# A hybrid recurrent and attention layer on one core: four gate units ahead of the seven-product pairs, another order of their sums, and more low parts made by DMA

## The chip, the core and the metric

The kernel runs on one core of a Trainium2 chip. The core has five engines with their own instruction streams: TensorE (PE, matmuls; PEld is its weight load), VectorE (DVE), ScalarE (ACT), GpSimd (POOL) and SyncE (SP), which here issues most DMAs. Each runs its instructions in the order in which they were written, and waits for others by semaphores. The metric is the device time of one execution in microseconds.

## The reference

One layer for 512 tokens of width 1024, all in float32:

```python
h = rmsnorm(x, norm_w)
proj = einsum('bsd,de->bse', h, w_in) + b_in      # 11272 columns
(mq, mk, mv, mi, mf, mo, mz, sq, sk, sv, sz, gates) = split(proj)
qk = silu(causal_conv4(concat([mq, mk])))          # mLSTM branch, 4 heads of 256
hm = rmsnorm(mlstm_chunkwise(q, k, v, log_i, log_f))
y_m = hm * sigmoid(mo) * silu(mz)
qs, ks = rmsnorm(sq), rmsnorm(sk)                  # stick-breaking attention, 8 heads of 128
y_s = stick_breaking_attention(qs, ks, sv) * silu(sz)
g_m, g_s = split(sigmoid(gates))
merged = g_m * (y_m @ w_proj_m) + g_s * (y_s @ w_proj_s)
out = x + merged @ w_out
```

Nearly all the work is the product of h with w_in, and the three products behind it.

## The kernel before, in words

**Float32 products.** Each operand is split into a high part, rounded to the format that TensorE takes (float32r), and a low part, the rest. A product is three matmuls, high by high, high by low and low by high (`mm3`, lines 93 to 96, and L963 in the pairs). Splitting a weight tile (`split`, L98) costs one ACT copy for `wh` (L99) and one DVE subtraction for `wl` (L100). Units marked `by_dma` make the low part otherwise: ACT writes `wh` (L126) and the negated weight into `wl` (L127), and POOL issues a DMA that adds the weight to it (L128). The buffer of the weight, `stg`, is then free only when that DMA has landed.

**Units.** The work of TensorE is a list of units that run one after the other. A full unit is 128 columns of a weight matrix by all tokens, or 256 rows by 512 columns, 24 matmuls of 512 columns. SP loads the weight of a unit four units ahead into one of three `stg` buffers; it is split two units ahead into one of three `wh` and of three `wl`. When a unit's products are done, the next iteration of the loop evacuates them from PSUM. Iteration c of the loop emits, in this order: the evacuation of unit c − 1; all that stands in the table `later` for c; the load of unit c + 4 and the split of unit c + 2; the first half of unit c's matmuls; steps of the attention and mLSTM heads that are under way, matmuls among them; the second half. This order is the program order on every engine, and nothing reorders it.

**The pairs.** v of both branches and k of set 0 come from two *pairs*. A pair computes two groups of 512 columns by the 2 × 2 block scheme that needs seven block products in place of eight (`Pair`, `Half`). Its blocks are X, Y, Z and V (each in two halves g); each product p has two half-units of 12 matmuls, which are split two half-units ahead as any unit is. The operands are sums of the blocks. Before, the sums are Y + V (`t3`, by DMA, L1010), X + Y (`t2`, L1014), Z + X (`t4`, L1018) and X − V (`t1`, L1022), the last three on DVE, and the products run in the order 1, 2, 6, 5, 7, 3, 4. Product 1 multiplies X, 2 Z, 6 X after X + Y, 5 X after X − V, 7 Y after Y + V, 3 V, 4 Z after Z + X. The same sums of h are the tiles `form`, made by DVE and ACT while x is normalised and in the first iterations (L905, L913, L914). Products 1, 6, 7 and 4 accumulate in bank a, 2 in c, 5 and 3 in b; ACT copies a bank into `u`, DVE adds a bank to the bias row into `dst` (L1043), and POOL adds `u` to it by DMA (L1046).

**The order of the groups before** (E = 32 is the first unit behind the pairs):

| units | what |
|---|---|
| 0 to 3 | q of attention set 0 |
| 4 to 17, 18 to 31 | pair 1 (v of set 1 and v of the mLSTM pair 1), pair 2 (v and k of set 0); half-units |
| 32 to 47 | z of set 0, q, k and z of set 1, four units each |
| 48 to 51 | first half of the merge gate g_m (GM), sigmoid on ACT, stored in DRAM (`gm_park`) |
| 52 to 67 | o, z, q, k of mLSTM pair 0 |
| 68 to 87 | o, z, v, q, k of mLSTM pair 1 |
| 88 to 99 | all eight units of the gate g_s (GS) and the second half of GM, kept in tiles |
| 100 to 115 | projections w_proj_s and w_proj_m, their 16 outputs times the gates |
| 116 to 129 | the output product, again by seven products |

Evacuations of q and k of a set are additions of the bias row on DVE (L387: `qraw`, `kraw`). k of mLSTM units and q units have a causal convolution on DVE (L729, L731, L737, L746) and two ACT steps; o and z units have one or two DVE instructions. The attention heads run beside units from E + 1 on: ACT exponentials (L504), POOL selects (L506), DVE scans (L512, L513) and transposes through DRAM.

`by_dma` are units 36 to 43 (q and k of set 1) and the last eight of w_proj_m, and the two half-units of product 1 in the first pair (L946 to 948).

Of the kernel before, what the change touches and what calls it, by code (L numbers as in the profile page):

```python
# [37 lines left out]
def tile_hybrid_layer(  # L38
# [931 lines left out]
    class Pair:  # L970

        def __init__(self, c1, c2, got1, got2):
# [36 lines left out]
        def t3(self, g):  # L1009
            nc.gpsimd.dma_start(out=self.raw["Y", g], in_=self.raw["V", g], accum_op=OP.add)  # L1010

        def t2(self, g):
            x, y = self.raw["X", g], self.raw["Y", g]
            nc.vector.tensor_tensor(x, x, y, op=OP.add)  # L1014

# [565 lines left out]
```

## Time and profile before

| | before |
|---|---|
| time, median of 3 runs | 699.28 us (699.22 to 702.11) |
| the profiled execution | 699.28 us, span 697.5 us |
| granted TensorE clock, mean | 0.995 |
| busy: PE, DVE, ACT, POOL | 677.6, 489.6, 374.9, 133.0 us |
| HBM read, written | 79.85, 15.79 MB |

A timeline row has its start in us, its duration in us, the engine, the line of the program, the instruction, its output and inputs, the shape and in brackets the idle time of the engine in front of it and what ended it. A window row has, behind its length, busy time and instructions of PE, PEld, DVE, ACT and POOL, the granted clock, the mean share of the DMA engines and GB/s. A group's row ends with its busy time and the mean duration in ns. Matmuls are pipelined, so each lasts longer than the step to the next.

### The profile page before, as it was taken

The page shows a single profiled execution, that of the slowest core. Times are in us where ns is not written, and L with a number is a line of the kernel's source. Part 1 is how long each engine was busy: PE and PEld are TensorE (multiplying, and loading weights), DVE is VectorE, ACT ScalarE, POOL GpSimd, SP SyncE. Part 2 cuts the span into 40 slices and gives each one's busy share as a digit, 9 for nine tenths or more (in the row PEclk, how much of TensorE's full clock was granted, in tenths as well). Part 3 has the DMA queues.
Part 4 walks back from the last instruction along what each step waited for, and adds up shares of the span by engine and source line. Part 5 has one row for each costly group of instructions (what it writes and reads, how often), then busy time and mean ns, then how long its engine had stood idle before and what let it go on. Part 6 is the DMA issues. An engine that isn't in the chain of part 4 may idle for free.

```text
span 697.5 us, 9279 instructions
## 1 busy us (share of the span) xinstructions
PE 677.6 (97%) x3114; PEld 560.4 (80%) x3114; DVE 489.6 (70%) x849; ACT 374.9 (54%) x705; POOL 133.0 (19%) x268
## 2 busy tenths in 40 slices
PE   8998999999979999999999999999999999999997
PEld 5876868788758888888887888888888888888876
DVE  6797596765496985698987545699643375445996
ACT  7567444666845645564355564444647453344451
POOL 4157203134621221210001031100002100111020
PEclk9999999999989999999999999999999999999999
DMA  7947948579788559475355424353523349679333
GB/s 247 309 100 223 267 113 204 161 162 253 196 209 254 147 175 249 127 187 98 86 117 144 113 76 135 107 150 91 134 78 90 91 145 298 190 169 220 125 81 101
DMA packets 131503, 111.97 MB, mean 161 GB/s; under 512 B 17098, under 2 KB 105572, under 8 KB 131456
## 3 DMA queue, kind: packets, MB, share of 16 engines
q1 hardware_dynamic: 125840, 95.53, 47.6%
q0 software_dynamic: 5472, 15.73, 12.0%
q8 instruction: 24, 0.39, 0.2%
q14 instruction: 23, 0.19, 0.1%
q10 hardware_dynamic: 144, 0.13, 0.1%
HBM read 79.85 MB, written 15.79 MB: 137 GB/s over the span
## 4 chain that ended last, share of the span: by engine, by line
PE 67%; DMA 7%; DVE 6%; issue 4%; ACT 3%; SPq 2%; POOL 0%; DVEq 0%; ACTq 0%; POOLq 0%
PE dps L94 19%; PE dps L95 19%; PE dps L96 19%; PE aps L95 3%; PE aps L96 3%; PE aps L94 3%; DMA stg<-in_w_in_dram 2%; DVE acc L731 2%; DMA Y<-V 2%; DMA t_d<-ty 1%; ACT sqj L404 1%; DMA wl<-stg 1%; DVE wl L100 1%; PE aps L840 1%; PE aps L842 1%
## 5 line engine op out<-in xcount | busy, mean ns | idle before, releaser
L94 PE MATMUL dps<-hh,wh 128*128 128x512 f32 x448 | 176.6, 394 | 4.2 <-DVE kraw L387 4.1
L96 PE MATMUL dps<-hh,wl 128*128 128x512 f32 x448 | 175.5, 392 | 0.5 <-DVE wl L100 0.5
L95 PE MATMUL dps<-hl,wh 128*128 128x512 f32 x448 | 175.4, 392 | 0.0
L100 DVE TENSOR_TENSOR wl<-stg,wh 128x1024 fp32r<-128x1024 f32 x68 | 83.2, 1223 | 59.9 <-ACT wh L99 59.7
L94 PEld LDWEIGHTS dps<-hh,wh 128*128 128x128 f32 x448 | 84.8, 189 | 21.7 <-issue 4.5
L96 PEld LDWEIGHTS dps<-hh,wl 128*128 128x128 f32 x448 | 84.7, 189 | 18.9 <-DVE wl L100 1.0
L95 PEld LDWEIGHTS dps<-hl,wh 128*128 128x128 f32 x448 | 84.8, 189 | 16.7
L99 ACT ACTIVATE wh<-stg 128x1024 fp32r<-128x1024 f32 x68 | 71.6, 1052 | 28.4 <-PE dps L95 20.6
L512 DVE TENSOR_TENSOR_SCAN om<-om 128x512 f32<-128x512 f32 (+3 forms) x32 | 27.0, 845 | 19.6 <-POOL om L506 19.6
L94 PE MATMUL dps<-wh,hh 128*128 128x512 f32 x96 | 37.6, 392 | 1.3 <-DVE qraw L387 1.3
L734 ACT ACTIVATE tmp<-acc 128x512 f32<-128x512 f32 x16 | 10.1, 633 | 52.3 <-DVE acc L731 52.3
L95 PE MATMUL dps<-wl,hh 128*128 128x512 f32 x96 | 37.5, 391 | 0.3 <-DMA wl<-stg 0.3
L96 PE MATMUL dps<-wh,hl 128*128 128x512 f32 x96 | 37.4, 390 | 0.0
L731 DVE SCALAR_TENSOR_TENSOR acc<-tmp,vec,acc 128x511 f32<-128x511 f32 (+2 forms) x48 | 36.0, 750 | 1.7
L126 ACT ACTIVATE wh<-stg 128x1024 fp32r<-128x1024 f32 x16 | 16.9, 1058 | 30.5 <-PE dps L95 15.5
L128 POOL DMA_DIRECT2D wl<-stg x16 | 14.1, 881 | 99.8 <-ACT wl L127 44.7
L506 POOL TENSOR_SCALAR_AFFINE_SELECT om<-om 128x128 f32<-128x128 f32 x32 | 16.4, 517 | 66.3 <-ACT om L504 49.2
L793 POOL TENSOR_SCALAR_AFFINE_SELECT w_all<-om 128x128 f32<-128x128 f32 x16 | 7.3, 491 | 108.3 <-DMA om<-rb_d 108.3
L94 PE MATMUL dps<-yh,wh 128*128 128x512 f32 x64 | 24.9, 389 | 0.0
L95 PE MATMUL dps<-yl,wh 128*128 128x512 f32 x64 | 24.9, 389 | 0.0
L96 PE MATMUL dps<-yh,wl 128*128 128x512 f32 x64 | 24.9, 389 | 0.0
L504 ACT ACTIVATE om<-aps,rq 128x512 f32<-128x512 f32 (+3 forms) x32 | 16.9, 528 | 12.7 <-PE aps L96 11.7
(302 smaller groups left out, 1555.2 us busy)
## 6 DMA issues: line engine op xcount, KB each, us to landing
stg<-in_w_in_dram SPq DMA_DIRECT2D x71, 512.0 KB
wl<-stg POOLq DMA_DIRECT2D x16, 512.0 KB, 5.9
a_d<-ay SPq DMA_DIRECT2D x8, 640.0 KB
az<-a_d SPq DMA_DIRECT2D x32, 160.0 KB
stg<-in_w_proj_s_dram SPq DMA_DIRECT2D x8, 512.0 KB
B<-in_w_out_dram SPq DMA_DIRECT2D x8, 512.0 KB
stg<-in_w_proj_m_dram SPq DMA_DIRECT2D x8, 512.0 KB
dst<-u POOLq DMA_DIRECT2D x12, 256.0 KB, 5.6
```

What stands on the lines that cost most here:

```text
L94: nc.tensor.matmul(ps, ah, bh, start=first, stop=False)
L95: nc.tensor.matmul(ps, ah, bl, start=False, stop=False)
L96: nc.tensor.matmul(ps, al, bh, start=False, stop=last)
L99: nc.scalar.activation(hi, src, AF.Copy)
L100: nc.vector.tensor_tensor(lo, src, hi.bitcast(F32), op=OP.subtract)
L126: nc.scalar.activation(self.wh, self.st, AF.Copy)
L128: nc.gpsimd.dma_start(out=self.wl, in_=self.st, accum_op=OP.add)
L504: nc.scalar.activation(om[:, 0:n], zp, AF.Sigmoid, scale=rn[:, h:h + 1])
L506: nc.gpsimd.affine_select(out=om[:, ts], in_=om[:, ts], compare_op=OP.is_gt, fill=1.0, base=0, channel_multiplier=1, pattern=[[-1, 128]])
L512: nc.vector.tensor_tensor_scan(back, back, back, 1.0, op0=OP.mult, op1=OP.bypass)
L731: nc.vector.scalar_tensor_tensor(acc[:, j:], t[:, 0:T - j], cw(3 - j, ch), acc[:, j:], op0=OP.mult, op1=OP.add)
L734: nc.scalar.activation(t, acc, AF.Sigmoid)
```

## The change

1. Four units (`FILL`), the first half of GS, stand between q of set 0 and the first pair. So the pairs are units 8 to 21 and 22 to 35, and E is 36. With them both pairs are loaded by a plan of due units, and the `form` sums and splits are made over iterations 2 to 7.
2. The pairs' products run in the order 1, 2, 5, 6, 7, 3, 4. The sums are X + Y (DVE, one iteration ahead of the pair), Y + V (DMA, one behind its start), X + V (DVE, three behind), Z + X (DVE, four behind). Product 5 takes X after the first sum, 6 after X + V. Products 6 and 7 now follow each other on bank a.
3. Product 1 of the first pair is split as all others.
4. The `by_dma` units are E + 4 to E + 19: z of set 1 and the first half of GM too. The low part of v of mLSTM pair 0, which returns from DRAM, is made in the same way.
5. z of mLSTM pair 0 alternates with q of that pair (`weave`): o, q, z, q, z, q, z, q, z, k.
6. All sixteen gate tiles are stored in DRAM behind their sigmoid (`park`) and come back at four places between the last gate unit and the eighth unit behind (`gate_back`). Buffers of that stretch change: the early splits of y_s go into `qk` tiles, two splits of y_m move to later units, and the loads and sums of the output product's weights move by one to four units.
7. The turn of q of set 0 goes from E − 9 to E − 6, the gates' scan from E + 24 to E + 26.

```diff
-E = 4 + 14 * PAIRS
+FILL = 4
+E = 4 + FILL + 14 * PAIRS
...
-GATES_PREP, GATES_START, GATES_SCAN = E - 3, E - 1, E + 24
+GATES_PREP, GATES_START, GATES_SCAN = E - 3, E - 1, E + 26
...
-            later.setdefault(E - 9, []).append(fn) if name == "q" else defer(2, fn)
+            later.setdefault(E - 6, []).append(fn) if name == "q" else defer(2, fn)
...
+            if not self.p:
+                nc.scalar.activation(vl, t, AF.Copy, scale=-1.0)
+                nc.gpsimd.dma_start(out=vl.rearrange("p h e -> p (h e)"), in_=t.rearrange("p h e -> p (h e)"), accum_op=OP.add)
+                return lambda: None
...
-            if self.pair.base == 4 and self.p == 1:
-                nc.scalar.activation(self.wh, x, AF.Copy)
-                nc.scalar.activation(self.wl, x, AF.Copy, scale=-1.0)
-                nc.gpsimd.dma_start(out=self.wl, in_=x, accum_op=OP.add)
-            else:
-                split(x, self.wh, self.wl)
+            split(x, self.wh, self.wl)
...
-            for p in (1, 2, 6, 5, 7, 3, 4):
+            for p in (1, 2, 5, 6, 7, 3, 4):
...
+                if first:
+                    plan = {"X": b - 6 + g, "Z": b - 3 + 3 * g, "V": b - 3 + g, "Y": b - 4 + g}
+                else:
+                    plan = {"X": b - 6 + g, "Z": b - 7 + 5 * g, "V": b - 3 + g, "Y": b - 6 + g}
...
-                self.at(b + g - 2, self.t3, g)
-                self.at(b + 1 + g, self.t2, g)
-                self.at(b + 3 + g, self.t4, g)
-                self.at(b + 4 + g, self.t1, g)
+                for n, (z, y, dma) in enumerate((("X", "Y", False), ("Y", "V", True),
+                                                   ("X", "V", False), ("Z", "X", False))):
+                    self.at(b + (-1, 1, 3, 4)[n] + g, self.sum, z, y, g, dma)
...
+    def park(dst, o, n=0):
+        def evac(ct, ps):
+            ct += n
+            t = blk("tmp", name="gpark")
+            nc.scalar.activation(t, ps, AF.Sigmoid, bias=bias(o + ct))
+            nc.sync.dma_start(dst[128 * ct:128 * ct + 128, :], t)
+        return evac
+
+    gs_park, gm_park = [dp.tile([D, T], F32, name=n) for n in ("gs_park", "gm_park")]
+    chan_group(w_in, C_GS, 512, h_mov, park(gs_park, 48))
...
+    weave(16, 0, 1, 2, 3, 8, 4, 9, 5, 10, 6, 11, 7, 12, 13, 14, 15)
...
-    gate_group(C_GS, 48, D, gs_tile)
-    gate_group(C_GM + 512, 44, 512, gm_late)
+    chan_group(w_in, C_GS + 512, 512, h_mov, park(gs_park, 48, 4))
+    chan_group(w_in, C_GM + 512, 512, h_mov, park(gm_park, 40, 4))
...
-    for un in units[n_proj - 8:] + units[E + 4:E + 12]:
+    for un in units[n_proj - 8:] + units[E + 4:E + 20]:
         un.by_dma = True
...
-    at_unit(n_gates + 3, gm_back)
+    at_unit(n_gates - 1, gate_back, gs_park, gs_t, 0, ("brow", "om", "om", "acc"))
+    for n in (0, 2):
+        at_unit(n_gates + 2, gate_back, gs_park, gs_t, 4 + n)
+        at_unit(n_gates + 4, gate_back, gm_park, gm_t, n)
+        at_unit(n_gates + 8, gate_back, gm_park, gm_t, 4 + n)
```

Three places of DVE's program are shown. Line numbers of the changed kernel differ: its split is L101, its sums are L1011.

The start of the first pair, before: `form` are the sums of h, `Z`, `X` the blocks, `dst` the first output.

```order
L100 TENSOR_TENSOR wl<-Z,wh 128x1024
L1014 TENSOR_TENSOR X<-X,Y 128x1024
L914 SCALAR_TENSOR_TENSOR form<-h_368,form 128x512
L914 SCALAR_TENSOR_TENSOR form<-h_349,form 128x512
L100 TENSOR_TENSOR wl<-Z,wh 128x1024
L1014 TENSOR_TENSOR X<-X,Y 128x1024
L914 SCALAR_TENSOR_TENSOR form<-h_352,form 128x512
L100 TENSOR_TENSOR wl<-X,wh 128x1024
L1018 TENSOR_TENSOR Z<-Z,X 128x1024
L100 TENSOR_TENSOR wl<-X,wh 128x1024
L1043 TENSOR_TENSOR dst<-prow,aps 128x512 x2
```

The same place now:

```order
L101 TENSOR_TENSOR wl<-X,wh 128x1024
L1011 TENSOR_TENSOR X<-X,Y 128x1024
L919 SCALAR_TENSOR_TENSOR form<-h_283,form 128x512
L919 SCALAR_TENSOR_TENSOR form<-h_286,form 128x512
L101 TENSOR_TENSOR wl<-X,wh 128x1024
L1011 TENSOR_TENSOR X<-X,Y 128x1024
L101 TENSOR_TENSOR wl<-Z,wh 128x1024 x2
L101 TENSOR_TENSOR wl<-X,wh 128x1024
L1011 TENSOR_TENSOR X<-X,V 128x1024
L101 TENSOR_TENSOR wl<-X,wh 128x1024
L1032 TENSOR_TENSOR dst<-prow,aps 128x512 x2
L1011 TENSOR_TENSOR Z<-Z,X 128x1024
```

X + Y stands ahead of both low parts of product 2's Z, and X + V behind the first low part of product 5's X.

The evacuation of k of set 1 (`kraw`), before: the rows above it are the last of head 1 (scans `om`, transposes `ay`) and two low parts of z units.

```order
L431 STREAM_TRANSPOSE ty<-qraw 128x8x32 x4
L100 TENSOR_TENSOR wl<-stg,wh 128x1024
L100 TENSOR_TENSOR atl<-az,ath 128x512
L100 TENSOR_TENSOR atl<-az,ath 128x384
L530 STREAM_TRANSPOSE ay<-a_all 128x4x32 x10
L512 SCALAR_TENSOR_TENSOR om<-om 128x256
L513 TENSOR_TENSOR a_all<-a_all,om 128x256
L512 SCALAR_TENSOR_TENSOR om<-om 128x384
L513 TENSOR_TENSOR a_all<-a_all,om 128x384
L100 TENSOR_TENSOR wl<-stg,wh 128x1024
L387 TENSOR_TENSOR kraw<-dps,brow 128x512 x4
```

The same place now:

```order
L432 STREAM_TRANSPOSE ty<-qraw 128x8x32 x4
L101 TENSOR_TENSOR atl<-az,ath 128x512
L101 TENSOR_TENSOR atl<-az,ath 128x384
L531 STREAM_TRANSPOSE ay<-a_all 128x4x32 x10
L513 SCALAR_TENSOR_TENSOR om<-om 128x256
L514 TENSOR_TENSOR a_all<-a_all,om 128x256
L513 SCALAR_TENSOR_TENSOR om<-om 128x384
L514 TENSOR_TENSOR a_all<-a_all,om 128x384
L388 TENSOR_TENSOR kraw<-dps,brow 128x512 x4
```

Both subtractions are gone from DVE; nothing else moved there.

Units of q of mLSTM pair 0 on DVE, before one after the other (`acc` and `tmp` are the convolution, `ys` a head's output):

```order
L100 TENSOR_TENSOR wl<-stg,wh 128x1024
L729 TENSOR_SCALAR acc<-tmp,vec 128x512
L731 SCALAR_TENSOR_TENSOR acc<-tmp,vec,acc 128x511
L731 SCALAR_TENSOR_TENSOR acc<-tmp,vec,acc 128x510
L731 SCALAR_TENSOR_TENSOR acc<-tmp,vec,acc 128x509
L746 TENSOR_TENSOR mqt<-tmp,mqt 128x512
L100 TENSOR_TENSOR atl<-az,ath 128x384
L737 SCALAR_TENSOR_TENSOR tmp<-acc,tmp 128x512
L100 TENSOR_TENSOR wl<-stg,wh 128x1024
```

Now with a z unit's two instructions (L718, L719) between:

```order
L730 TENSOR_SCALAR acc<-tmp,vec 128x512
L732 SCALAR_TENSOR_TENSOR acc<-tmp,vec,acc 128x511
L732 SCALAR_TENSOR_TENSOR acc<-tmp,vec,acc 128x510
L732 SCALAR_TENSOR_TENSOR acc<-tmp,vec,acc 128x509
L747 TENSOR_TENSOR mqt<-tmp,mqt 128x512
L101 TENSOR_TENSOR atl<-az,ath 128x512
L101 TENSOR_TENSOR atl<-az,ath 128x384
L718 SCALAR_TENSOR_TENSOR tmp<-dps,bvec,tmp 128x512
L719 SCALAR_TENSOR_TENSOR ym<-tmp,vec,ym 128x512
L101 TENSOR_TENSOR wl<-stg,wh 128x1024
```

Between two convolutions now stand a z unit's evacuation and its low part.

More of the change, by code (lines that the diff above doesn't have):

```diff
@@ L1007, in load, with sum @@
             nc.sync.dma_start(t, w_in[r:r + 256, c:c + 512].rearrange("(k p) c -> p k c", p=128))
[L1009 to L1014, printed above, removed]
-        def t4(self, g):
-            z, x = self.raw["Z", g], self.raw["X", g]
-            nc.vector.tensor_tensor(z, z, x, op=OP.add)
-        def t1(self, g):
-            x, v = self.raw["X", g], self.raw["V", g]
-            nc.vector.tensor_tensor(x, x, v, op=OP.subtract)
+        def sum(self, z, y, g, dma):
+            z, y = self.raw[z, g], self.raw[y, g]
+            if dma:
+                nc.gpsimd.dma_start(out=z, in_=y, accum_op=OP.add)
+            else:
+                nc.vector.tensor_tensor(z, z, y, op=OP.add)
         def rows(self):
@@ L1075, in at_unit @@
         later.setdefault(c, []).append(lambda: fn(*a))
-    at_unit(1, units[4].split)
-    for f in (5, 7, 6):
-        for i in range(2):
-            at_unit(2, form_sum, f, i)
-    for f, c in ((6, (3, 4)), (5, (4, 5)), (7, (5, 6)), (3, (9, 10))):
+    for n, c in enumerate((2, 2, 2, 2, 3, 3)):
+        at_unit(c, form_sum, (5, 7, 6)[n // 2], n % 2)
+    for f, c in ((5, (4, 4)), (6, (5, 5)), (7, (6, 6)), (3, (7, 7))):
         for i in range(2):
@@ L1094, in tile_hybrid_layer, with weave @@
     sets[1].z_group()
-    gm_park = dp.tile([512, T], F32, name="gm_park")
-    def gm_early(ct, ps):
-        t = blk("tmp", name="gmp")
-        nc.scalar.activation(t, ps, AF.Sigmoid, bias=bias(40 + ct))
-        nc.sync.dma_start(gm_park[128 * ct:128 * ct + 128, :], t)
-    chan_group(w_in, C_GM, 512, h_mov, gm_early)
+    chan_group(w_in, C_GM, 512, h_mov, park(gm_park, 40))
+    def weave(n, *order):
+        b = len(units) - n
+        units[b:] = [units[b + i] for i in order]
     pairs[0].o_group()
@@ L1111, in tile_hybrid_layer, with gate_back @@
     pairs[1].qk_group("k", C_MK, 8)
-    gs_t, gm_t = [], [None] * 8
-    def gs_tile(ct):
-        if ct < 4:
-            tag = ("brow", "om", "om", "acc")[ct]
-            gs_t.append(blk(tag, shape=(516 if tag == "om" else 512,), name="gs")[:, 0:512])
-        elif ct % 2 == 0:
-            gs_t.extend(two("qk", name="gs"))
-        return gs_t[ct]
-    def gm_back():
-        for n in range(2):
-            t = blk("qk", F32, (2, 512), name="gm")
-            nc.sync.dma_start(t, gm_park[256 * n:256 * n + 256, :].rearrange("(i p) t -> p i t", p=128))
-            for i in range(2):
-                gm_t[2 * n + i] = t[:, i, :]
-    def gm_late(ct):
-        if ct % 2 == 0:
-            gm_t[4 + ct:6 + ct] = two("qk", name="gm")
-        return gm_t[4 + ct]
-    def gate_group(c0, o, n, tile_of):
-        def evac(ct, ps):
-            nc.scalar.activation(tile_of(ct), ps, AF.Sigmoid, bias=bias(o + ct))
-        chan_group(w_in, c0, n, h_mov, evac)
-    gate_group(C_GS, 48, D, gs_tile)
-    gate_group(C_GM + 512, 44, 512, gm_late)
+    gs_t, gm_t = [None] * 8, [None] * 8
+    def gate_back(src, dst, n, tags=None):
+        if tags:
+            for i, tag in enumerate(tags):
+                dst[n + i] = blk(tag, shape=(516 if tag == "om" else 512,), name="gback")[:, 0:512]
+                nc.sync.dma_start(dst[n + i], src[128 * (n + i):128 * (n + i) + 128, :])
+        else:
+            t = blk("qk", F32, (2, 512), name="gback")
+            nc.sync.dma_start(t, src[128 * n:128 * n + 256, :].rearrange("(i p) t -> p i t", p=128))
+            for i in range(2):
+                dst[n + i] = t[:, i, :]
+    chan_group(w_in, C_GS + 512, 512, h_mov, park(gs_park, 48, 4))
+    chan_group(w_in, C_GM + 512, 512, h_mov, park(gm_park, 40, 4))
     n_gates = len(units)
@@ L1486, in tile_hybrid_layer @@
     for k in range(8):
-        later.setdefault(n_gates + 3 + k // 2, []).append(
+        later.setdefault(n_gates + (3 + k // 2 if k < 6 else 8), []).append(
             y_late(y_m, ymp, k, k) if k < 5 else y_own(k))
@@ L1534, in tile_hybrid_layer @@
             x_turn(2)
-            units[5].split()
         for g in list(act):
```

34 lines of the change are left out of this document (14 added, 20 removed).

## The prediction

> **What bounds the kernel now.** I read the page's busy shares and its chain of waits first.
>
> ```profile
> PE 677.6 (97%) x3114; PEld 560.4 (80%) x3114; DVE 489.6 (70%) x849; ACT 374.9 (54%) x705; POOL 133.0 (19%) x268
> PE 67%; DMA 7%; DVE 6%; issue 4%; ACT 3%; SPq 2%; POOL 0%; DVEq 0%; ACTq 0%; POOLq 0%
> ```
>
> TensorE is busy for 97% of the span, and the change leaves it the same products. So only the time in which it waits can be won. The timeline of PE gives every such wait behind the start-up (in brackets: the idle time and what ended it); the first and third row stand before and behind one of them, and the row at 263.92, which waits for nothing, is used further on.
>
> ```profile
> 43.08 0.39 PE L963 MATMUL aps<-wh,hh 128*128 128x512 f32 x1
> 43.90 0.50 PE L963 MATMUL aps<-wl,hh 128*128 128x512 f32 x1 [0.44 <-DVE wl L100]
> 44.24 0.40 PE L963 MATMUL aps<-wh,hl 128*128 128x512 f32 x1
> ...
> 52.53 0.50 PE L963 MATMUL aps<-wh,form 128*128 128x512 f32 x1 [0.24 <-ACT wh L99]
> 54.85 0.50 PE L963 MATMUL aps<-wl,form 128*128 128x512 f32 x1 [1.82 <-DVE wl L100]
> 58.40 0.50 PE L963 MATMUL aps<-wl,form 128*128 128x512 f32 x1 [0.53 <-DVE wl L100]
> 62.43 0.50 PE L963 MATMUL dps<-wl,form 128*128 128x512 f32 x1 [0.76 <-DVE wl L100]
> 95.83 0.50 PE L963 MATMUL aps<-wh,form 128*128 128x512 f32 x1 [0.26 <-ACT wh L99]
> 97.09 0.50 PE L963 MATMUL aps<-wl,form 128*128 128x512 f32 x1 [0.76 <-DVE wl L100]
> 100.67 0.50 PE L963 MATMUL aps<-wl,form 128*128 128x512 f32 x1 [0.56 <-DVE wl L100]
> 132.42 0.33 PE L481 MATMUL aps<-ident,dst 128*128 128x128 f32 x1 [0.80 <-DVE dst L419]
> 133.20 0.55 PE L481 MATMUL aps<-ident,dst 128*128 128x128 f32 x3 [0.46 <-DVE dst L419]
> 176.18 0.50 PE L94 MATMUL dps<-wh,hh 128*128 128x512 f32 x1 [1.30 <-DVE qraw L387]
> 195.81 0.50 PE L95 MATMUL dps<-wl,hh 128*128 128x512 f32 x1 [0.27 <-DMA wl<-stg]
> 205.40 0.77 PE L94 MATMUL dps<-hh,wh 128*128 128x512 f32 x1 [4.09 <-DVE kraw L387]
> 263.92 0.39 PE L94 MATMUL dps<-hh,wh 128*128 128x512 f32 x1
> 380.80 0.50 PE L96 MATMUL dps<-hh,wl 128*128 128x512 f32 x1 [0.52 <-DVE wl L100]
> ```
>
> A wait costs more than its idle time. Matmuls follow each other by some 0.23 us (44.24 − 43.90 is 0.34); around the wait of 0.44 us two steps take 44.24 − 43.08 = 1.16 in place of 0.46, so 0.70 are lost: the idle time and 0.26 more. The long wait at 205.40 costs clock too, which the view by short windows shows (PEclk is the column behind the engines).
>
> ```profile
> 203.00:204.00 1.00, 0.00 (x0) 0.00 (x0) 1.00 (x2) 0.00 (x0) 0.00 (x0) 0.83 1.07 313
> ...
> 210.00:211.00 1.00, 1.00 (x5) 0.82 (x4) 0.85 (x1) 0.00 (x0) 0.02 (x1) 0.76 1.14 342
> ```
>
> All rows between them have 0.50. A mean of 0.83 is half speed from 203.66 on, and 0.76 ends it at 210.48. The idle time began at 205.40 − 4.09 = 201.31, so the clock fell 2.35 us into it. From 205.40 to 210.48 half speed cost 5.08 / 2 = 2.5 us. With 0.26 for each wait, the losses are: first pair 3.79 + 5 × 0.26 = 5.1; second pair 1.58 + 0.78 = 2.4; at head 0, 1.26 + 0.52 = 1.8; before k of set 1, 1.56; the DMA's, 0.53; at 205.40, 4.09 + 0.26 + 2.5 = 6.85; at 380.80, 0.78. Together 19.0 us. The profiled execution took 699.28 us, which is the median of the runs itself, so the sum is made against 699.28 and its least possible end is 680.3.
>
> **The pairs.** Two rows of the chain say what the pairs and head 0 wait for besides DVE, two windows and two groups what DVE and PE have to do there.
>
> ```profile
> 75.58 11.96 DMA Y<-V
> 114.72 9.38 DMA stg<-in_w_in_dram
> ```
>
> ```profile
> 40.00:60.00 20.00, 16.98 (x71) 12.56 (x70) 18.45 (x21) 12.22 (x36) 16.34 (x7) 1.00 0.32 95
> 580.00:600.00 20.00, 20.00 (x90) 16.56 (x89) 12.60 (x16) 7.26 (x11) 0.00 (x0) 1.00 0.87 275
> ```
>
> ```profile
> L1043 DVE TENSOR_TENSOR dst<-prow,aps 128x512 f32<-128x512 f32 x8 | 5.1, 684 | 0.0
> L1022 DVE TENSOR_TENSOR X<-X,V 128x1024 f32<-128x1024 f32 x4 | 4.9, 1225 | 0.0
> ```
>
> Before, Y + V (the DMA of 11.96 us) stands ahead of X + Y, on which products 6, 5 and 4 depend, and DVE is busy 18.45 of 20 us around 50. After, X + Y needs loads alone, and Y + V goes out in the second half-unit of the pair and is read by the ninth. 90 matmuls in 20 us are 0.222 each, so a half-unit of 12 is 2.67 us; its split runs two half-units ahead, which leaves five of them, 13.4 us, for a transfer of 11.96. The fullest half-unit for DVE is now the fifth: two adds into dst, two sums and one subtraction, 2 × 0.68 + 3 × 1.22 = 5.0 us at most, against the two half-units (5.33 us) by which splits run ahead. So DVE just keeps up if it enters it without a lag. In the first pair four squares of a q norm stand ahead of ACT's copy there, and DVE has done two subtractions more than before, since the first pair's low parts are no longer made by DMA. I take 1.0 us of stalls for the first pair (bounds: 0, and the 5.1 of before with those two subtractions, 7.5) and 0.3 for the second (0 to 2.4). **Gain: 4.1 + 2.1.**
>
> The four gate units ahead of the pairs are the same TensorE work at another place: 24 matmuls of a unit and one subtraction of 1.2 us each, on a DVE that a full unit (5.3 us) leaves idle most of the time; their sigmoids (one ACT instruction for each) go into the two tmp buffers and from there to DRAM by SP. At head 0 the load of 9.38 us came late behind the second pair's loads, and the k norm's scale behind it on ACT, in order. The pair's loads now stand at other units and less together; I take 0.3 of the 1.8 as left (0 to 1.8). **Gain: 1.5.**
>
> **Sixteen low parts by DMA.** Before k of set 1 is evacuated, DVE works without a gap from 189 us; four rows of it:
>
> ```profile
> 196.52 1.19 DVE L100 TENSOR_TENSOR wl<-stg,wh 128x1024 fp32r<-128x1024 f32 x1
> 197.63 1.15 DVE L100 TENSOR_TENSOR atl<-az,ath 128x512 fp32r<-128x512 f32 x2
> ...
> 203.44 1.22 DVE L100 TENSOR_TENSOR wl<-stg,wh 128x1024 fp32r<-128x1024 f32 x1
> 204.57 1.88 DVE L387 TENSOR_TENSOR kraw<-dps,brow 128x512 f32<-128x512 f32 x3
> ```
>
> The two subtractions are low parts of the first two z units behind it, and both leave DVE. They take 1.11 and 1.13 us of its time (197.63 − 196.52 and 204.57 − 203.44), so kraw starts at 202.33 and PE idles 4.09 − 2.24 = 1.85 us. That ends 0.50 us ahead of the point at which the clock fell, and the wait of 1.82 us at 54.85 stands in a window with the clock at 1.00. What is left is 1.85 + 0.26 = 2.1 us. **Gain: 4.7.** The wait at 176.18 has nothing moved ahead of it and stays.
>
> [...]
>
> The price is on ACT and POOL: the second copy, and the issue of the transfer.
>
> ```profile
> L127 ACT ACTIVATE wl<-stg 128x1024 fp32r<-128x1024 f32 x16 | 16.7, 1044 | 0.0
> L128 POOL DMA_DIRECT2D wl<-stg x16: 850/864/947, 139.9 to 641.0; - x16
> DMA to landing us min/median/max: 4.5/6.1/8.5
> ```
>
> The four low parts of pair 0's v go the same way, two of the pairs' no longer do, so POOL issues ten more transfers. One low part takes 2 × 1.04 + 0.86 + 6.1 = 9.0 us from its split, at most 2.9 + 8.5 = 11.4. The eight new units ran from 205.40 to 263.92 (the row of that time is the first matmul behind them), without the 2.5 us of lost clock 7.0 each, so two of them are 14.0 us of lead. The transfers hide, by 2.6 us even with the longest of these rows. The buffer stg comes free only on landing, and three of them serve all: load, copies, issue and landing have three units, 21.0 us, against 9.38 + 2.1 + 0.9 + 8.5 = 20.9. I take the one late wait of before (0.53) and 0.8 for the new ones (bounds: 0 and the rival C below). **Loss: 0.8.**
>
> **z woven with q.** In the second half of the program DVE lags behind four convolutions in a row, and one wait (0.78) comes of it. Placing a z unit, which gives DVE two instructions beside its low part where a q unit gives five, between q units takes that lag out in steps; I take half, with 0 and 0.78 as ends. **Gain: 0.4.**
>
> **Gates parked in DRAM.** Sixteen tiles of 256 KB cross to DRAM and back in place of four: 3 MB more stored, over the whole program, and 3 MB more loaded, within nine units behind the last gate unit, where the projections' weights are loaded too.
>
> ```profile
> 20.00:40.00 20.00, 20.00 (x94) 16.39 (x93) 16.02 (x37) 13.13 (x30) 3.66 (x4) 1.00 1.06 305
> 600.00:620.00 20.00, 20.00 (x90) 16.58 (x89) 6.25 (x9) 8.55 (x9) 3.37 (x4) 1.00 0.75 184
> 620.00:640.00 20.00, 20.00 (x90) 16.57 (x89) 12.32 (x20) 8.84 (x11) 2.73 (x4) 1.00 0.91 197
> ```
>
> At 305 GB/s, the fullest window, 3.15 MB take 10.3 us of all DMA engines. The windows from 580 to 640 have shares of 0.87, 0.75 and 0.91, so 0.47 × 20 = 9.4 us are free there. The loads of the last weights start one to four units later and make room, so that it need cost nothing; if none of the free time can be used it costs 10.3. I take what is over, 0.9. **Loss: 0.9.**
>
> **The sum:** 4.1 + 2.1 + 1.5 + 4.7 + 0.4 − 0.8 − 0.9 = 11.1, and 699.28 − 11.1 = **688.2 us**.
>
> **The rivals.** *A: the clock still falls.* ACT makes each z unit's second copy (1.04 us) in the same stretch, in order, ahead of the exponentials that DVE's scans wait for. If that delays kraw by over 0.50 us, PE idles past 2.35 us and half speed follows, 2.5 us, with up to 1.0 us of wait: 688.2 + 3.5 = 691.7. For it: the margin of 0.50 is small beside the 2.24 on which it rests. Against it: at 189 to 204 DVE ran without a pause, so it was DVE's own work that was late.
>
> *B: the pairs' stalls only move.* The sums are as many as before, DVE has two subtractions more in the first pair, and products 6 and 7 now share a bank back to back, with a copy by ACT between them that PE must wait for. If 6.2 of the pairs' gain is gone, 688.2 + 6.2 = 694.4. For it: 18.45 of 20 us busy in the first pair. Against it: the chain went through Y + V, and the change takes it off the way to products 5 and 6.
>
> *C, on the other side: the three stg buffers become the bound in the eight new units.* With a landing as the pairs' (11.96 us) in place of 8.5, the round of load, copies, issue and landing is 9.38 + 3.0 + 11.96 = 24.3 us for three units of 21.0: 1.1 us lost a unit, 8.8 in all, 697.0. It decides from a round of 26.5 us on, 2.2 us above these longest rows: there (26.5 − 21.0) / 3 × 8 = 14.7 us go and the result passes 702.8; with 27.5 us 17.3 are lost and it is **705.5**. For it: SP waits for the buffer in order, so loads of other tiles (the transposes' round through DRAM, the parked v) come later as well, and gate stores are added to its queue. Against it: eight units in a row already work so before the change, with one wait of 0.27.
>
> [...]
>
> **How the numbers follow.** About 0.5%, 3.5 us, is what a measurement of this kernel can tell from no change: faster is below 695.8, slower above 702.8. The forecast has 0.47 (its own range 684 to 692, by the pairs' and the buffers' bounds), A 0.14, B 0.19, C 0.14 (half of it above 702.8), and 0.06 lie with the crowded end of the program, up to 688.2 + 9.4 = 697.6. Faster: 0.47 + 0.14, 0.14 of B (the rest where losses at the buffers join it) and 0.04 of the last: 0.79. Slower: half of C and a little of B: 0.08. Same: 0.13. The range goes from 681, all but nothing of the 19.0 left, to 699.
>
> **What would show it.** X + Y of each pair ending while its product 1 runs; Y<-V landing without anyone waiting; no idle over 1 us within the pairs. DVE going from its transposes to kraw without a low part between, PE idle there near 1.85, the granted clock 1.00 in that window. 24 issues of wl<-stg by POOL in place of 16, and landings under 9 us. No new idle time in the last 130 us. The forecast is wrong if PE waits for "DMA wl<-stg" in the GM units, if the clock shows 0.50 near k, or if waits for DVE's low parts sum to more than 3 us in the pairs.

## The result and the profile after

The changed kernel takes 694.93 us (median of 20 runs, 692.87 to 700.82) against 699.29 us (20 runs) of the kernel before: a ratio of 0.9941, with a 95% interval of 0.9927 to 0.9955. It is 4.4 us faster; 11.1 were forecast, and 694.93 lies within the range of 681 to 699 but at less than half of the gain. The profiled execution took 695.85 us, 3.4 less than that of before.

The timeline of PE of the changed kernel has these waits behind the start-up; it answers the list in the prediction (L101 is now the split, L388 the evacuation of `kraw`, L482 the first matmul of head 0).

```profile
68.72 0.50 PE L963 MATMUL aps<-wl,form 128*128 128x512 f32 x1 [0.50 <-DVE wl L101]
75.72 0.50 PE L963 MATMUL dps<-wl,form 128*128 128x512 f32 x1 [1.25 <-DVE wl L101]
149.88 0.33 PE L482 MATMUL aps<-ident,dst 128*128 128x128 f32 x1 [2.47 <-DVE dst L420]
150.66 0.55 PE L482 MATMUL aps<-ident,dst 128*128 128x128 f32 x3 [0.46 <-DVE dst L420]
193.66 0.50 PE L95 MATMUL dps<-wh,hh 128*128 128x512 f32 x1 [1.30 <-DVE qraw L388]
213.29 0.50 PE L96 MATMUL dps<-wl,hh 128*128 128x512 f32 x1 [0.28 <-DMA wl<-stg]
220.41 0.47 PE L95 MATMUL dps<-hh,wh 128*128 128x512 f32 x1 [1.61 <-DVE kraw L388]
233.47 0.50 PE L97 MATMUL dps<-hh,wl 128*128 128x512 f32 x1 [0.19 <-DMA wl<-stg]
259.78 0.50 PE L96 MATMUL aps<-ktt,qtt 128*128 128x512 f32 x1 [0.52 <-DVE ktt L101]
301.21 0.50 PE L96 MATMUL aps<-ktt,qtt 128*128 128x512 f32 x1 [1.92 <-DVE ktt L101]
607.70 0.50 PE L97 MATMUL dps<-yh,wl 128*128 128x512 f32 x1 [0.25 <-DMA wl<-stg]
```

The second pair has no wait left, the first one 1.75 us; `kraw` waits 1.61 in place of 4.09. But head 0 waits longer than before (2.47 and 0.46 in place of 0.80 and 0.46), and two waits are new, both in front of the attention heads' first product (`ktt`, at 259.78 and 301.21). With 0.26 us for each wait, as in the prediction, against its losses of before:

| place | before | after | forecast for after |
|---|---|---|---|
| pairs | 7.5 | 2.3 | 1.3 |
| head 0 | 1.8 | 3.5 | 0.3 |
| before k of set 1 (`qraw`) | 1.6 | 1.6 | 1.6 |
| low parts by DMA near 213 and 233 | 0.5 | 1.0 | 1.3 |
| `kraw` with its clock | 6.85 | 1.9 | 2.1 |
| `ktt` with its clock | 0 | 4.7 | 0 |
| behind the convolutions | 0.8 | 0 | 0.4 |
| the end | 0 | 0.5 | 0.9 |
| sum | 19.0 | 15.5 | 7.9 |

The sums fall by 3.5 us, the profiled executions by 3.4. The clock part of `ktt` is from the view by windows of the changed kernel:

```profile
302.00:303.00 1.00, 1.00 (x8) 0.89 (x7) 1.00 (x2) 0.00 (x0) 0.00 (x0) 0.80 0.00 0
...
306.00:307.00 1.00, 1.00 (x5) 0.83 (x5) 0.00 (x0) 0.00 (x0) 0.00 (x0) 0.99 0.01 3
```

Half speed lasts from 302.60 (a mean of 0.80) to 306.02 (0.99), 3.42 us, and costs half of that, 1.7. Two misses make up the difference: 3.2 us at head 0 and 4.7 at `ktt`.

**Head 0.** The chain of waits of the changed kernel ahead of 149.88:

```profile
132.16 8.16 DMA stg<-in_w_in_dram
140.40 1.07 ACT wh L100
142.36 4.18 DMA stg<-in_w_in_dram
146.65 1.07 ACT wh L100
149.74 0.88 DVE dst L420 x4
```

Two weight loads came late, one after the other, ACT waited for each in order, and the scale of k's norm (`dst`) on DVE came behind. The timeline of SP says why:

```profile
128.07 0.60 SPq L120 DMA_DIRECT2D stg<-in_w_in_dram  x1
128.72 3.34 SPq L440 DMA_DIRECT2D t_d<-ty  x4
132.16 0.57 SPq L120 DMA_DIRECT2D stg<-in_w_in_dram  x1
139.01 3.31 SPq L445 DMA_DIRECT2D tz<-t_d  x4
142.36 0.58 SPq L120 DMA_DIRECT2D stg<-in_w_in_dram  x1
```

L440 and L445 are the turn of q of set 0, which the change moves from E − 9 to E − 6: four stores to DRAM and four loads back, which wait until the stores have landed. From 132.7 to 139.0 SP issued nothing: it stood in front of the four loads of L445, and the weight load behind them was issued at 142.36.

**`ktt`.** Ahead of 301.21 the chain is made of the same kind of piece:

```profile
240.07 11.08 DMA stg<-in_w_in_dram
260.64 8.30 DMA stg<-in_w_in_dram
273.81 5.99 DMA vback<-v_park
294.02 1.04 ACT wh L100
```

and the view of waits of the changed kernel names what ACT waited for before its copies of weights (total in us, times, longest), over the whole program:

```profile
ACT wh L100 <- DMA stg<-in_w_in_dram: 12.8, 5, 4.2
ACT wh L127 <- DMA stg<-in_w_in_dram: 4.7, 3, 2.4
```

Between 230 and 303 us it is 6.4 us in two waits of the first kind and all of the second.

So my theory after the result was: SP's order at head 0; and at `ktt` the sixteen low parts by DMA, which hold the three `stg` buffers until they land, so that loads of later units start late, ACT waits for them in order, and the heads' steps behind ACT come late on DVE. The rivals: full DMA engines in both places, or the gate stores and the returning v in SP's queue.

### The profile page after: what moved, and what is told of

Read it like the earlier page. It is cut to its first block, busy times and chain, and to the rows that moved or that the text cites. A ratio compares the mean times of both kernels' runs of the same rounds, so it can differ in the third digit from the quotient of the medians.

```text
span 693.7 us, 9384 instructions
## 1 busy us (share of the span) xinstructions
PE 676.1 (97%) x3114; PEld 559.9 (81%) x3114; DVE 480.6 (69%) x839; ACT 383.5 (55%) x715; POOL 130.0 (19%) x278
## 4 chain that ended last, share of the span: by engine, by line
PE 66%; DMA 13%; DVE 6%; issue 6%; ACT 5%; POOL 2%; SPq 2%; ACTq 0%; DVEq 0%; POOLq 0%
PE dps L97 16%; PE dps L95 16%; PE dps L96 16%; DMA stg<-in_w_in_dram 5%; PE dps L963 4%; DMA wl<-stg 3%; DMA vback<-v_park 2%; PE aps L963 2%; PE aps L96 2%; PE aps L97 2%; DMA stg<-in_w_proj_m_dram 2%; PE aps L95 2%; ACT sqj L405 1%; DVE wl L101 1%; PE dps L1438 1%
## 5 line engine op out<-in xcount | busy, mean ns | idle before, releaser
L101 DVE TENSOR_TENSOR wl<-stg,wh 128x1024 fp32r<-128x1024 f32 x60 | 73.4, 1224 | 55.9 <-ACT wh L100 55.8
L129 POOL DMA_DIRECT2D wl<-stg x24 | 21.1, 879 | 103.1 <-ACT wl L128 72.7
L128 ACT ACTIVATE wl<-stg 128x1024 fp32r<-128x1024 f32 x24 | 25.1, 1047 | 0.0
L101 DVE TENSOR_TENSOR atl<-az,ath 128x384 fp32r<-128x384 f32 (+1 forms) x24 | 13.9, 607 | 15.1 <-ACT ath L100 8.7
```

Of the source, the lines that this page charges most:

```text
L101: nc.vector.tensor_tensor(lo, src, hi.bitcast(F32), op=OP.subtract)
L128: nc.scalar.activation(self.wl, self.st, AF.Copy, scale=-1.0)
L129: nc.gpsimd.dma_start(out=self.wl, in_=self.st, accum_op=OP.add)
```

## The experiments

All times are medians, of four runs for most kernels, with the ratio to runs of the kernel before on the same chip. The intervals of two of these kernels that lie within some 2 us of each other mostly overlap; there the waits in the profiles carry the reading, and not the difference of the medians.

### 1. The turn of q back at E − 9

```diff
-            later.setdefault(E - 6, []).append(fn) if name == "q" else defer(2, fn)
+            later.setdefault(E - 9, []).append(fn) if name == "q" else defer(2, fn)
```

> The changed kernel with one edit undone: the turn of q of set 0 goes back from E - 6 to E - 9. Theory (SP's queue): the turn's sixteen small DMAs, eight of which wait for the others to land, stand in SP's queue ahead of the weight loads of the units behind the pairs, ACT waits for those loads in order, and the scale of k's norm is late behind it. Then the wait of PE for 'DVE dst' at head 0 (2.47 + 0.46 us of idle time in the changed kernel's profile) falls to that of the kernel before (0.80 + 0.46) or below, and the time falls by 1.7 to 3.4 us against the changed kernel's 694.9, to 691.5 to 693.2. Rival (the pair's loads or the DMA engines' load make those loads late, wherever the turn stands): the wait stays at 2.5 or more, the time at 694.9.

690.90 us, ratio 0.9872 (0.9854 to 0.989): 4.0 less than the changed kernel. No wait at head 0 is left, of 2.93. That is the theory, and more than it promised: the two waits for `ktt` are still there, but of other lengths and without the clock's fall, which had cost 1.7 us.

```profile
217.29 0.47 PE L95 MATMUL dps<-hh,wh 128*128 128x512 f32 x1 [1.86 <-DVE kraw L388]
257.35 0.50 PE L96 MATMUL aps<-ktt,qtt 128*128 128x512 f32 x1 [1.70 <-DVE ktt L101]
297.68 0.50 PE L96 MATMUL aps<-ktt,qtt 128*128 128x512 f32 x1 [0.83 <-DVE ktt L101]
```

### 2. Ten units' low parts by DMA in place of sixteen

```diff
-    for un in units[n_proj - 8:] + units[E + 4:E + 20]:
+    for un in units[n_proj - 8:] + units[E + 4:E + 14]:
```

> The changed kernel with low parts by DMA for E + 4 to E + 13 only, ten units in place of sixteen: the first two z units keep it, the other two and the four gate units get DVE's subtraction back. Theory (stg): the low-part DMAs hold the three stg buffers until they land and fill the DMA engines, so the later loads start late, ACT waits for them in order, and the heads' rows come late on DVE. Then the waits at 233, 260 and 301 us (0.19, 0.52 and 1.92 us idle, with half clock behind the last) go, kraw stays at some 1.6 us, and the time falls by 4 to 5 us to 690 to 691. Rival (the parked v's return and the gate stores in SP's queue make the wait at 301 us): that wait stays at about 1.9 us, and the time at 694 to 695.

692.73 us, ratio 0.9904 (0.987 to 0.9937), with a profiled execution of 690.65. The waits for `ktt` are gone, though the returning v and the gate stores still stand in SP's queue, so that rival falls as a cause by itself; `kraw` waits for 1.71 us. The median fell by 2.2 us, less than expected; the profiled execution fell by 5.2 against that of the changed kernel (695.85) although half speed struck at head 0, which is still late here:

```profile
149.20 0.48 PE L482 MATMUL aps<-ident,dst 128*128 128x128 f32 x1 [2.17 <-DVE dst L420]
```

### 3. Both edits

> Both edits together: the turn of q at E - 9 and ten units' low parts by DMA. If both causes are as said and do not touch each other, the gains add up to 6 to 8 us: 687 to 689, about the forecast of 688.2, with waits of PE behind the start-up of 7 us or less. If they share one cause (full DMA engines), the two together gain no more than the better of them, 690 to 691.

688.42 us, ratio 0.9836 (0.9814 to 0.9858): 6.5 less than the changed kernel, about the sum of the first two (4.0 and 2.2), and at the forecast of 688.2. The two causes are separate. Its waits behind the start-up:

```profile
68.50 0.50 PE L963 MATMUL aps<-wl,form 128*128 128x512 f32 x1 [0.41 <-DVE wl L101]
75.50 0.50 PE L963 MATMUL dps<-wl,form 128*128 128x512 f32 x1 [1.22 <-DVE wl L101]
190.11 0.50 PE L95 MATMUL dps<-wh,hh 128*128 128x512 f32 x1 [1.30 <-DVE qraw L388]
216.86 0.47 PE L95 MATMUL dps<-hh,wh 128*128 128x512 f32 x1 [2.08 <-DVE kraw L388]
599.35 0.50 PE L97 MATMUL dps<-yh,wl 128*128 128x512 f32 x1 [0.56 <-DMA wl<-stg]
638.54 0.50 PE L97 MATMUL dps<-yh,wl 128*128 128x512 f32 x1 [0.55 <-DMA wl<-stg]
```

### 4. The kernel before with ten units' low parts by DMA

```diff
-    for un in units[n_proj - 8:] + units[E + 4:E + 12]:
+    for un in units[n_proj - 8:] + units[E + 4:E + 14]:
```

> The kernel before with one edit: low parts by DMA for E + 4 to E + 13, two units more. It tests the step on kraw alone: the forecast's step has PE's idle time in front of k of set 1 at 1.85 us in place of 4.09, the clock at 1.00 throughout, and a gain of 4.7 us: 694.6. Rival A: ACT's two more copies delay the scans, PE idles over 2.35 us and the clock falls: 698 or more.

694.82 us, ratio 0.9928 (0.991 to 0.9946). The forecast of 694.6 holds: one line on two units brings all of the gain at `kraw`, and by itself as much as the whole change. PE waits 1.30 us there, and the clock stays at 1.00:

```profile
203.40 0.47 PE L94 MATMUL dps<-hh,wh 128*128 128x512 f32 x1 [1.30 <-DVE kraw L387]
```

### 5, 9, 11, 12. Four stg buffers, at a price

The first edit with a fourth `stg` buffer tells whether the low parts hurt by the buffers they hold or by the DMA engines. Its space was taken from the unused columns of `vh`:

```diff
-    BUFS = {"stg": 3, ...
+    BUFS = {"stg": 4, ...
-            vh = blk("vh", FR, (576,))
+            vh = blk("vh", FR, (520,))
```

> The changed kernel with the turn of q at E - 9, all sixteen low parts by DMA, and four stg buffers in place of three (the columns of vh that nothing uses are given up for them). It tells the two halves of the theory on stg apart. If the low-part DMAs hurt since they hold the buffer of a later load, that load no longer waits, the waits for ktt (1.70 and 0.83 us idle with three buffers) go, and the time is 688 to 688.5 in place of 690.9. If they hurt since the DMA engines are full between 200 and 300 us, the waits for ktt stay at 2 us or more together and the time at 690 to 691.

702.66 us, ratio 1.0044 (1.0029 to 1.0059). No wait for `ktt` was left, and still it was 12 us slower than with three buffers: with the clock at 1.00 and no wait, 87 or 88 matmuls ran in 20 us in place of 90, in most windows that hold nothing but matmuls of 512 columns. Three runs went after that. The ninth had 528 columns, the eleventh 544, and the twelfth 528 columns and *three* buffers, in the kernel of the tenth experiment (below).

> The kernel of the fifth experiment again, but a row of vh has 528 columns in place of 520 (576 in the changed kernel), so that each buffer behind it starts at a multiple of 64 bytes again (520 x 4 = 2080 is none, 528 x 4 = 2112 and 576 x 4 = 2304 are). In the fifth experiment the matmuls followed each other 87 times in 20 us in place of 90, everywhere, with the clock at 1.00. If that came of where the buffers start, it is 90 again, and the waits decide: with four stg buffers no wait for ktt, so 688 to 689 in place of 690.9 with three. If it came of the fourth buffer, it stays at 87 and 702.

> Sixteen low parts by DMA and four stg buffers as in the fifth and ninth experiment, but a row of vh has 544 columns (2176 bytes, a multiple of 128; 528 gave 2112, no such multiple, 576 gives 2304). If the matmuls' slower pace (0.233 in place of 0.227 us) comes of where buffers start, it is 0.227 again; then without a wait for ktt the time is 688 to 689 in place of 690.9 with three buffers (theory on stg), or 690 to 691 with those waits (full DMA engines). If it comes of the fourth stg buffer itself, the pace stays at 0.233 and the time at 700 or more.

> The kernel of the tenth experiment (three stg buffers, 685.9) with 528 columns in a row of vh in place of 576, nothing else. If where the buffers start slows the matmuls, the pace is 0.233 us and the time about 698 to 700; if the fourth buffer did, the pace is 0.227 and the time 685 to 687.

700.27 us (ratio 1.0016, 0.9996 to 1.0036), 700.13 us (1.0019, 1.0007 to 1.003) and 696.44 us (0.9955, 0.9939 to 0.9971). The twelfth decides it: against 685.86 us of the same kernel with 576 columns it loses 10.6 us, with the same three buffers. One window of each, first 576 columns, then 528:

```profile
480.00:500.00 20.00, 20.00 (x90) 16.57 (x89) 18.43 (x27) 10.16 (x15) 0.00 (x0) 1.00 0.33 88
```

```profile
480.00:500.00 20.00, 20.00 (x87) 16.10 (x86) 18.43 (x26) 10.28 (x16) 0.00 (x0) 1.00 0.45 123
```

PE is busy all the time in both, at the same clock, with three matmuls less. From 420 to 580 us it is 771 against 761. So it is the shorter rows. The matmuls of this window read `hh`, `hl`, `wh` and `wl` and never `vh`, so the likely way is by where the rows make other buffers start; that was argued, not shown. My guess of 64 bytes (ninth) and that of 128 (eleventh) both fell: 520, 528 and 544 columns are 2080, 2112 and 2176 bytes, 576 are 2304, of which only the last is a multiple of 256. That this is what counts was not tried by itself, and which operand suffers stays open.

### 13. Four stg buffers at the full pace

The space now comes from two small tiles of the gates in one buffer of 256 bytes; `vh` keeps 576 columns.

```diff
-    c_lag = [cst.tile([128, TB, NH], F32, name=f"c_lag{k}") for k in range(TB)]
-    gst = cst.tile([128, KT, 8], F32, name="gst")
+    gst2 = cst.tile([128, 64], F32, name="gst")
+    gst = gst2.rearrange("p (k c) -> p k c", k=KT)
+    c_lag = [gst2[:, 16 * k:16 * k + 16].rearrange("p (j h) -> p j h", j=TB) for k in range(TB)]
```

> The kernel of the first experiment (q's turn at E - 9, sixteen low parts by DMA) with four stg buffers, at the full pace of the matmuls: the space now comes from two small tiles of the gates that share one buffer (256 bytes less), and a row of vh has its 576 columns again, so that no buffer starts otherwise than at the same place within 256 bytes. Theory on stg (a low part's DMA holds the buffer of a later load): no wait for ktt, 688 to 689 in place of 690.9. Theory of full DMA engines: waits for ktt of 2 us or more together, 690 to 691. The pace should be 90 matmuls in 20 us; if it is 87 again, the fourth buffer has a part in the slow pace after all.

689.86 us, ratio 0.9854 (0.984 to 0.9869); 90 matmuls in 20 us again. The waits for `ktt` are gone, while the DMA engines are as full as before (the last but one number of the row is their share; it is 1.04 in this window in experiment 1 too):

```profile
240.00:260.00 20.00, 20.00 (x102) 17.06 (x101) 15.34 (x31) 13.81 (x26) 8.79 (x21) 1.00 1.04 263
```

So it is the round through the buffers, and not what the engines can move: with one buffer more the loads start early enough. How much of a late load was a buffer still held by a low part, and how much its own later landing, this does not separate. Between 200 and 310 us the median landing of a load, where the profile shows it, was 6.1 us in the changed kernel and 4.2 with ten low parts (experiment 2). And the time fell by 1.0 us only, not by the 2 to 3 of those waits. Other waits grew, all for low parts that landed late (the median landing went from 6.3 us in experiment 1 to 7.6):

```profile
204.66 0.50 PE L96 MATMUL dps<-wl,hh 128*128 128x512 f32 x1 [0.88 <-DMA wl<-stg]
230.66 0.50 PE L97 MATMUL dps<-hh,wl 128*128 128x512 f32 x1 [0.65 <-DMA wl<-stg]
601.48 0.50 PE L97 MATMUL dps<-yh,wl 128*128 128x512 f32 x1 [1.41 <-DMA wl<-stg]
640.84 0.50 PE L97 MATMUL dps<-yh,wl 128*128 128x512 f32 x1 [0.98 <-DMA wl<-stg]
```

The rival has that much of it: with loads no longer held back, the full engines are the next bound.

### 6. The old order of the pairs' sums

The kernel of experiment 3 with products 1, 2, 6, 5, 7, 3, 4 and the old sums; the four gate units stay ahead.

```diff
-            for p in (1, 2, 5, 6, 7, 3, 4):
+            for p in (1, 2, 6, 5, 7, 3, 4):
...
-                for n, (z, y, dma) in enumerate((("X", "Y", False), ("Y", "V", True),
-                                                   ("X", "V", False), ("Z", "X", False))):
-                    self.at(b + (-1, 1, 3, 4)[n] + g, self.sum, z, y, g, dma)
+                for n, (z, y, dma) in enumerate((("Y", "V", True), ("X", "Y", False),
+                                                   ("Z", "X", False), ("X", "V", False))):
+                    self.at(b + (-2, 1, 3, 4)[n] + g, self.sum, z, y, g, dma, n == 3)
```

(the last sum subtracts; the loads of Y and V stand where the old order needs them)

> The better kernel of the third experiment (q's turn at E - 9, ten units' low parts by DMA; 688.4) with the pairs' sums and products in the order of the kernel before (Y + V by DMA ahead of the pair, then X + Y, Z + X, X - V; products 1, 2, 6, 5, 7, 3, 4), the four gate units still ahead. The forecast put 6.2 us of gain on the pairs without saying which of the two edits brings it. If it is the order of the sums, waits of the kind of before come back in both pairs, 3 to 6 us, and the time is 691 to 694. If it is the four gate units (loads and form splits in time), it stays within 1 us of 688.4.

690.93 us, ratio 0.9885 (0.9858 to 0.9912): 2.5 more than experiment 3. It falls between the two expectations. Waits came back in both pairs, as these four with one of 0.46 at 69.33 and one of 0.25 at 75.08:

```profile
76.34 0.50 PE L963 MATMUL aps<-wl,form 128*128 128x512 f32 x1 [0.76 <-DVE wl L101]
79.89 0.50 PE L963 MATMUL aps<-wl,form 128*128 128x512 f32 x1 [0.49 <-DVE wl L101]
115.85 0.50 PE L963 MATMUL aps<-wl,form 128*128 128x512 f32 x1 [0.31 <-DVE wl L101]
119.43 0.50 PE L963 MATMUL aps<-wl,form 128*128 128x512 f32 x1 [0.55 <-DVE wl L101]
```

With 2.82 us idle and 6 × 0.26 the pairs lose 4.4 here, 7.5 before and 2.2 in experiment 3. So of the pairs' gain the order of the sums has 2.2, and the rest, about 3, is left for the gate units ahead with their loads and forms; that part was not run alone.

### 7. Without the weave

```diff
-    weave(16, 0, 1, 2, 3, 8, 4, 9, 5, 10, 6, 11, 7, 12, 13, 14, 15)
```

> The kernel of the third experiment without the weave: z of mLSTM pair 0 stands as one group ahead of q again. The forecast gave the weave 0.4 us (0 to 0.78): a wait of PE for a low part on DVE comes back near 375 us with up to 0.5 us idle, and the time is 688.4 to 689.2. A rival: with fewer subtractions on DVE the weave brings nothing, no wait comes back, 688.4.

693.07 us, ratio 0.9911 (0.9882 to 0.994): 4.6 more than experiment 3, far over the 0.78 at which I had set the end. The wait near 397 is as expected (0.30 us), but the loss is elsewhere:

```profile
352.70 0.43 PE L95 MATMUL aps<-ath,vh 128*128 128x256 f32 x1 [2.21 <-ACT ath L100]
```

Ahead of it the chain runs through DVE from 342.6 to 346.9 with the scan of the mLSTM gates (L645 to L654), then through a convolution to 351.6, and ACT's copy for the attention head waits in order behind that. With the weave, in experiment 3, no wait stands there. The clock falls too, from 352.90 to 356.32, which costs 1.7 us; and it falls once more in this profile, from 219.78 to 223.18 behind a wait of 1.91 us for `kraw`, which is no work of the weave. So the 4.6 us are not the weave's alone: the one run of this kernel at a mean clock of 1.000 took 691.32 us, the profiled one of experiment 3 at 1.000 took 687.54, 3.8 less.

### 8. Four low parts at the end back on DVE

```diff
-    for un in units[n_proj - 8:] + units[E + 4:E + 14]:
+    for un in units[n_proj - 4:] + units[E + 4:E + 14]:
```

> The kernel of the third experiment with the low parts of the first four units of w_proj_m by DVE; the last four stay with DMA. If the waits for 'DMA wl<-stg' at the end of the program (0.56 and 0.55 us idle) come of the crowded DMA engines and the landing, the first goes and the second gets smaller, and the time falls by 0.8 to 1.6 us to 687 to 687.6. If DVE has no room there (it also evacuates and merges), waits for 'DVE wl' take their place and the time does not fall.

686.54 us, ratio 0.9814 (0.9795 to 0.9833): 1.9 less than experiment 3, whose interval overlaps. Both waits for `wl<-stg` at the end are gone; one of 0.21 us for DVE is left there.

### 10. The q norm under the gate units

Experiment 8 with the squares earlier:

```diff
-                    later.setdefault(6 + 2 * tb, []).append(lambda: self.norm(name, tb, t))
+                    later.setdefault(5 + tb, []).append(lambda: self.norm(name, tb, t))
```

> The kernel of the eighth experiment with the squares of the q norm of set 0 in iterations 5 to 8, under the gate units, in place of 6, 8, 10 and 12. The forecast put the first pair's wait (1.2 us idle at product 6) down to four squares that ACT makes ahead of the copy in the fifth half-unit. If so, the wait falls to 0.3 us or less and the time by 0.9 to 1.3 us to 685.2 to 685.7. A rival: DVE's own five instructions there are the bound; then it stays at 1.2 and 686.5.

685.86 us, ratio 0.9807 (0.9787 to 0.9826), the fastest kernel of this study. No wait is left in either pair, so it was the squares ahead of ACT's copy, not DVE's five instructions. The median fell by 0.7 only, less than the 1.2 us idle and not clear of the spread of four runs; a wait of 0.46 us came up at head 0 (at 146.30).

### 14. The fastest kernel with sixteen low parts and four buffers

> The kernel of the tenth experiment (685.9) with all sixteen low parts by DMA again and four stg buffers. If four buffers free the sixteen low parts of their cost and DVE gains by having six subtractions less, 684 to 686; if the landing itself is late for some units, waits for 'DMA wl<-stg' between 210 and 260 us cost 1 to 2 us, 686.5 to 688.

687.04 us, ratio 0.9819 (0.9803 to 0.9836): not faster, and the 1.2 us more are within the intervals. A wait of 1.07 us for `wl<-stg` stands at 235.99 and one of 0.52 at 637.90. So sixteen low parts and four buffers win nothing over ten and three.

## Why the prediction was wrong

**The bound and the losses** were read rightly: the waits of PE as counted above fall by 3.5 us, the profiled executions by 3.4.

**The pairs**: the mechanism was right. The second pair lost all its waits; the first kept 2.3 us for which 1.0 was taken, at the place named, and for the reason named (experiment 10). No wait of PE comes from Y + V any more.

**`kraw`** was right: 1.61 us in place of 1.85, the clock at 1.00, and 4.7 us in the kernel before by this edit alone (699.28 − 4.7 = 694.6 forecast, 694.82 measured). But the margin of 0.50 us to the clock's fall was no margin, and that the clock stayed up was in part luck: in experiment 7 it fell at this very place, behind a wait of 1.91 us, far under the 2.35 that rival A was built on (see the last section).

**Head 0 is where the prediction failed first**: "I take 0.3 of the 1.8 as left". This step goes by the pair's loads, which the change spreads, and leaves out the turn of q, which it moves: sixteen DMAs, eight of them waiting, now stand in SP's queue right ahead of the loads on which head 0 hangs. It lost 1.7 us more than before where a gain of 1.5 was forecast. Experiment 1 gives back 4.0 us in all.

**The second failure is in the part on the low parts by DMA, "I take ... 0.8 for the new ones"**. The sum there had the buffers' round at 20.9 us of 21.0 and took that for enough. It is no slack at all: loads took up to 11.08 us in place of 9.38, with the DMA engines fuller; one window of both kernels, before, then after (the changed kernel is some 15 us later in its units here; from 255 to 275 us its share is 0.92):

```profile
240.00:260.00 20.00, 20.00 (x97) 16.96 (x96) 17.00 (x37) 11.17 (x20) 4.16 (x15) 1.00 0.49 149
```

```profile
240.00:260.00 20.00, 19.48 (x96) 16.30 (x95) 13.86 (x28) 14.01 (x23) 6.52 (x15) 1.00 1.03 261
```

Rival C had the mechanism, but looked for it in the wrong wait. I let PE wait for `wl`; that cost 0.19 us. What came late was the next unit's load, and the one who waited was ACT, in order, with the heads' rows behind. That is 4.7 us with the clock in the profiled execution; in the medians ten low parts in place of sixteen give back 2.2 (experiment 2). The 0.8 was too little by either, and C's 8.8, by the longest rows, too much. Half of C's chance was put on a kernel slower than before, where it never came.

**The weave** was mis-sized: 0.4 forecast, some 4 us by experiment 7 (3.8 to 4.6, the second with clock), in a kernel with the other changes. The forecast went by the one wait of before and not by what the changed order would do without the weave.

**The end** was about right: 0.5 in the profile for 0.9, and up to 1.9 by experiment 8. The crowd there was low parts by DMA as much as gates.

With the two failures taken out, in experiment 3, the kernel takes 688.42 for the forecast 688.2. That the two totals meet is in part luck: the pairs kept 2.2 us for 1.3 and the end 1.6 for 0.9, while the low parts by DMA near 213 and 233 and the convolutions cost next to nothing for 1.3 and 0.4.

## What to carry to other kernels

A step that is moved takes its DMAs along: look at the queue that it now stands in, and at which load is behind it, before asking what the engines do. A low part or a copy that moves to DMA frees an engine and holds a buffer: add up the buffer's whole round (load, copies, issue, landing, with the landing as it will be on fuller engines; here a load took up to 11.08 us in place of 9.38), and take a sum that just fits (here 20.9 of 21.0 us) for a loss; the wait may come out at an engine that only stands in order behind the load (here ACT, for up to 4.2 us). And count first how few units need it: two of the eight added here brought the gain at `kraw`.

## What the runs showed of the hardware

**In these runs a wait's length alone did not decide whether the clock fell.** Waits of 2.47 us (the changed kernel, head 0) and 2.08 us (experiment 3) kept the clock at 1.00, while one of 1.92 us (the changed kernel, at 301.21) cost half speed, which began 1.4 us after PE had gone on. So did one of 2.17 us in experiment 2 (window by window):

```profile
149.00:150.00 1.00, 0.49 (x2) 0.20 (x2) 1.00 (x6) 0.46 (x1) 0.00 (x0) 0.57 0.54 90
152.00:153.00 1.00, 1.00 (x5) 0.82 (x4) 0.85 (x2) 0.00 (x0) 0.00 (x0) 0.72 0.35 37
```

Half speed lasted 3.42 us there (149.14 to 152.56) and in the changed kernel (302.60 to 306.02), and in the kernel before 6.82 (203.66 to 210.48), twice as long.

The two falls of experiment 7 begin at 219.78 and 352.90, by these rows (0.89 and 0.95 are means of full and half speed):

```profile
219.00:220.00 1.00, 1.00 (x5) 0.82 (x4) 1.00 (x3) 0.90 (x6) 0.00 (x0) 0.89 1.02 204
352.00:353.00 1.00, 0.30 (x1) 0.19 (x1) 0.43 (x2) 1.00 (x3) 0.00 (x0) 0.95 1.14 357
```

That is 133.12 us apart, 39 times 3.413, a step that agrees with those lengths of half speed. In the 3.41 us ahead of each of these five falls PE had been idle for 2.34 us (the kernel before, at 203.66), 1.92 (the changed kernel, at 302.60), 2.11 (experiment 2, at 149.14), and 1.91 and 2.21 (experiment 7). Counted in steps of 3.413 us from its fall, no other stretch of the kernel before or of the changed kernel, at full clock and behind the start-up, held more than 1.61 us. The edge of such a stretch, 45 steps ahead of the fall at 302.60, lies at 149.00 and cuts the changed kernel's wait of 2.47 us (147.41 to 149.88) into 1.59 and 0.88. So, as an estimate from the traces of these two kernels, a wait of about 2 us cost clock or not by where it fell against such steps. What sets them was not shown.

That this is why the changed kernel's twenty runs spread over 8 us (with mean clocks from 0.988, in the slowest, to 1.000) while experiment 10's four spread over 2.2 is likely, and was not shown.

**In these kernels the length of a tile's rows cost TensorE's pace**: rows of 2304 bytes in a tile that five buffers share gave 90 matmuls in 20 us of 512-column matmuls, and 2080, 2112 or 2176 bytes mostly gave 87 to 89. In the twelfth experiment this cost 10.6 us, 1.5% of the time. The clock and the waits show nothing of it; only the count of matmuls in a window without waits does. That it comes of where other buffers start is the likely reason, and was not shown.
